# Attention of a decoder trunk: batched norms with their offset in PSUM, values as the standing operand in the last two tiles, and a split last projection

## The chip, the cores and the metric

The kernel runs on one core of a Trainium2 chip. The metric is the device time of one execution in microseconds; lower is better. The engines are named as in the profile: PE is TensorE, PEld its loads of the standing operand, DVE is VectorE, ACT is ScalarE, POOL is GpSimd, SP is SyncE. In a PE row the first operand after the arrow is the standing one or the moving one as the program lists it; what stands is said in words where it matters.

## The reference

Two layers over 1024 positions of width 1024. Layer 0 is sparse attention, layer 1 a gated linear recurrence; a dense feed-forward follows each. The change lies in the attention, in the norm behind it and at the entry to the first feed-forward.

```python
def attend_block(args):
    qb, qib, wb, start = args
    ...
    rel = jax.nn.relu(jnp.einsum('bqhd,bsd->bhqs', qib, k_idx))
    score = jnp.einsum('bqh,bhqs->bqs', wb, rel).astype(jnp.float32)
    ...
    _, sel = lax.top_k(score, topk)
    ...
    logits = jnp.einsum('bqgrd,bqkgd->bqgrk', qg, k_sel).astype(jnp.float32) * (ATT_HEAD_DIM ** -0.5)
    ...
    p = jax.nn.softmax(logits, axis=-1).astype(dt)
    o = jnp.einsum('bqgrk,bqkgd->bqgrd', p, v_sel)
...
    return out @ w_o
...
    h = layer_norm(DEEPNORM_ALPHA * h + mix, ln_g[layer, 0], ln_b[layer, 0])
    ffn = swiglu(h, ffn_w_gate[layer], ffn_w_up[layer], ffn_w_down[layer])
    h = layer_norm(DEEPNORM_ALPHA * h + ffn, ln_g[layer, 1], ln_b[layer, 1])
```

## The kernel before

The positions are cut into 8 tiles of 128 queries. `att_main` goes over them as j = 0 to 7; a tile has two groups (gi = 0, 1) of 8 heads, which share one key and one value head of 64 channels. Tile j attends to j + 1 blocks of 128 keys. The chosen keys (the top 256 of the index scores) enter as a bias of large numbers on the logits.

For each head, `head` does this:

- **Logits.** Two matmuls per 512 (or 384, 448) keys give `L` in PSUM (L1597). DVE adds the bias and takes the row minimum in one instruction (L1599), ACT takes the exponential and its sum (L1601).
- **Transposes.** PE turns the 128x128 blocks of `p`, up to four into one PSUM bank `T` (L1607). ACT copies the bank to SBUF as `pT` (L1609).
- **Product.** For each key block `pT` stands and the 64 channels of the values move (L1612), and the sum stays in bank `O`. The product is in plain fp32, which the trace shows as two PE instructions per product.

After 8 heads, `heads_out` divides by the sums (L1625, DVE), turns the 128x512 result (L1634, PE) and splits it into a rounded part and a rest (L222 on ACT, L223 on DVE), `oth` and `otl`. `att_out` is the output projection: two halves of 512 columns, for each 8 blocks of the contraction with three matmuls (`mm3`, L103 to L105), 48 in all, into bank `W`; then DVE adds the scaled residual (L1647). Then comes the norm of that tile: `layer_norm([j], *gb, True)`, of which the order is

```python
            if spread:
                nc.scalar.activation(r, r, AF.Identity, bias=mr[:, i : i + 1], scale=rs[:, i : i + 1])
                nc.gpsimd.tensor_tensor(r, r, g, op=ALU.mult)
                v.tensor_tensor(r, r, b, op=ALU.add)
```

that is, DVE takes the statistics (L128, L129) and an inverse root in eleven 128x1 operations (`rsqrt`, L111 to L116) and one more (L135), ACT scales and shifts (L139), POOL multiplies by the gain (L140), DVE adds the offset (L141).

`heads_out` and `att_out` are not called at once: they are put into the list `late` with a count, and `tick`, called after each head, lowers the counts and calls what has come to 0. A projection started by `tick` goes on two blocks of the contraction per head. `LATE[j]` is the count for the projection of tile j. Beside that, the index scores and the search for the top keys of later tiles (`index`, `find`, up to L1502) are mixed into the heads of tiles 0 to 5 by the numbers in `PLAN`; for tiles 6 and 7 these are zero. The tile framework fixes the buffers and the waits; each engine then runs its instructions in order. PSUM has two banks each for `L`, `T`, `O`, and the pools of banks `W` and `I` (the index scores).

Behind the last projection stands the entry to the feed-forward, `enter`: it turns the normed rows with PE (L339, four 128x128 blocks per bank `Y`), splits them (L457, L458) and starts the gate and up matmuls. For later feed-forwards there is already a form in which the norm's offset is added on PE: a matmul of the small tiles `blocks` and `off` onto the turned bank (L341), and at the end of that feed-forward the same offset for the residual (`plus`, L726).

## Time and profile before

| | |
|---|---|
| median of 3 runs | 2673.97 us (2669.08 to 2676.54) |
| profiled execution, own time | 2682.22 us |
| its span, first to last instruction | 2680.4 us |
| PE busy in it | 2542.1 us (95%) |
| DVE busy | 1978.4 us (74%) |
| ACT busy | 1124.5 us (42%) |
| POOL busy | 266.7 us (10%) |
| mean granted clock of PE | 0.972 |

The profiled execution is 8.25 us longer than the median. Busy time of PE counts matmuls that overlap in the pipeline at the length that the profile gives each, so a busy PE is not a PE at its peak; how far apart matmuls start (the pitch) is read from the timeline. In the trace of this kernel the first exponential of tile 0 is at 256 us, of tile 1 at 288, tile 5 at 474, tile 6 at 537, tile 7 at 601; the last matmul of the projection is issued at 691.6 and the entry to the feed-forward runs from there to 739.

### The profile page before, as it was taken

The numbers are of one execution on the slowest core, as the hardware profiler recorded it, in microseconds if no ns is written. First come the engines' busy times: TensorE is split into PE (matmuls) and PEld (weight loads), VectorE is DVE, ScalarE is ACT, GpSimd is POOL, SyncE is SP. The second block draws the span as 40 slices with busy tenths as digits, with TensorE's granted clock in tenths as the row PEclk, the third lists the DMA queues.
The fourth block names the chain that finished last, engine by engine and source line by source line (L and its number), as shares of the span: only waits on it lengthen the run. The fifth ranks groups of instructions, "written<-read, shape, count | busy, mean of one in ns | idle before, by whom it ended". The sixth has DMA issues, their size and how long they took to land.

```text
span 2680.4 us, 37329 instructions
## 1 busy us (share of the span) xinstructions
PE 2542.1 (95%) x13242; PEld 2115.5 (79%) x13242; DVE 1978.4 (74%) x4025; ACT 1124.5 (42%) x2192; POOL 266.7 (10%) x350
## 2 busy tenths in 40 slices
PE   8977799999899999999999999999899999999998
PEld 7765678888787888888878888888678878888786
DVE  6599889644577877656678888887786777665667
ACT  4576667555432223334444333333344323333431
POOL 1323522220000000000001221111000000000000
PEclk9987799999899999999999999999899999999999
DMA  3213210000166663276631111112525663326853
GB/s 132 79 56 128 92 36 28 25 33 17 40 203 227 227 207 112 93 244 209 209 134 48 40 71 56 40 52 87 185 107 187 223 229 111 118 86 214 271 181 126
DMA packets 160338, 332.59 MB, mean 124 GB/s; under 512 B 16712, under 2 KB 48152, under 8 KB 152472
## 3 DMA queue, kind: packets, MB, share of 16 engines
q1 hardware_dynamic: 160152, 330.21, 36.6%
q8 instruction: 104, 1.70, 0.3%
q14 instruction: 82, 0.67, 0.1%
HBM read 231.02 MB, written 99.09 MB: 123 GB/s over the span
## 4 chain that ended last, share of the span: by engine, by line
PE 61%; DVE 20%; DMA 11%; issue 4%; ACT 3%; SPq 1%; POOL 1%; DVEq 0%; ACTq 0%; POOLq 0%
PE M L103 8%; PE M L104 8%; PE M L105 7%; PE Y L103 6%; PE Y L105 6%; PE Y L104 5%; PE O L1612 4%; DMA wdt<-in_wd_dram 4%; DMA t4q<-wdt 3%; DVE w L458 3%; PE Y L1036 2%; PE L L1597 2%; PE T L1607 2%; DVE wdt L567 2%; PE Y L339 1%
## 5 line engine op out<-in xcount | busy, mean ns | idle before, releaser
L457 ACT CAST w<-raw 128x512 fp32r<-128x512 f32 (+1 forms) x373 | 288.1, 774 | 479.8 <-PE M L105 253.2
L458 DVE TENSOR_TENSOR w<-raw,w 128x512 fp32r<-128x512 f32 (+1 forms) x373 | 327.8, 882 | 167.0 <-ACT w L457 165.6
L103 PE MATMUL M<-x,w 128*128 128x512 f32 (+1 forms) x1120 | 435.4, 389 | 8.2 <-DVE e L491 6.4
L104 PE MATMUL M<-x,w 128*128 128x512 f32 (+1 forms) x1120 | 431.4, 385 | 0.0
L105 PE MATMUL M<-x,w 128*128 128x512 f32 (+1 forms) x1120 | 428.1, 383 | 3.5 <-DVE w L458 3.5
L103 PEld LDWEIGHTS M<-x,w 128*128 128x128 f32 x1120 | 212.7, 190 | 49.4 <-DVE e L491 8.5
L103 PE MATMUL Y<-x,w 128*128 128x512 f32 (+1 forms) x644 | 245.7, 381 | 6.1 <-DVE e L491 5.5
L105 PE MATMUL Y<-x,w 128*128 128x512 f32 (+1 forms) x644 | 245.5, 381 | 2.1 <-DVE w L458 2.1
L105 PEld LDWEIGHTS M<-x,w 128*128 128x128 f32 x1120 | 212.5, 190 | 42.7 <-DVE w L458 3.9
L104 PE MATMUL Y<-x,w 128*128 128x512 f32 (+1 forms) x644 | 245.4, 381 | 0.0
L457 ACT CAST w<-s 128x512 fp32r<-128x512 f32 x180 | 111.7, 621 | 312.2 <-PE M L105 99.0
L104 PEld LDWEIGHTS M<-x,w 128*128 128x128 f32 x1120 | 212.9, 190 | 36.5
L1612 PEld LDWEIGHTS O<-vv,pT 128*128 128x128 f32 x1152 | 148.1, 199 | 27.2 <-ACT pT L1609 24.1
L1612 PE MATMUL O<-vv,pT 128*128 128x64 f32 x1152 | 154.7, 282 | 5.1 <-ACT pT L1609 4.0
L458 DVE TENSOR_TENSOR w<-s,w 128x512 fp32r<-128x512 f32 x180 | 124.4, 691 | 42.6 <-ACT w L457 42.1
L103 PEld LDWEIGHTS Y<-x,w 128*128 128x128 f32 x644 | 121.5, 189 | 31.1 <-DVE e L491 7.2
L105 PEld LDWEIGHTS Y<-x,w 128*128 128x128 f32 x644 | 121.5, 189 | 25.6 <-DVE w L458 2.5
L104 PEld LDWEIGHTS Y<-x,w 128*128 128x128 f32 x644 | 121.4, 189 | 23.0
L1597 PE MATMUL L<-ks,qt 128*128 128x512 f32 (+5 forms) x384 | 115.7, 391 | 20.7 <-DVE nm L1599 19.6
L567 DVE TENSOR_TENSOR wdt<-wdt 128x512 f32<-128x512 f32 x104 | 71.8, 691 | 79.1 <-DMA wdt<-in_wd_dram 54.5
L1609 ACT COPY pT<-T 128x512 f32<-128x512 f32 (+3 forms) x192 | 85.2, 478 | 85.7 <-PE T L1607 84.9
L1601 ACT ACTIVATE p<-p,nm 128x128 f32<-128x128 f32 (+7 forms) x128 | 99.3, 777 | 51.0 <-DVE nm L1599 50.5
(426 smaller groups left out, 5484.5 us busy)
## 6 DMA issues: line engine op xcount, KB each, us to landing
raw<-in_wgu_dram SPq DMA_DIRECT2D x44, 1024.0 KB
wdt<-in_wd_dram SPq DMA_DIRECT2D x44, 512.0 KB
raw<-in_wd_dram SPq DMA_DIRECT2D x66, 256.0 KB
raw<-in_hw_dram SPq DMA_DIRECT2D x16, 1024.0 KB
qr<-qd SPq DMA_DIRECT2D x64, 128.0 KB
t5q<-wdt SPq DMA_DIRECT2D x26, 256.0 KB
t7q<-wdt SPq DMA_DIRECT2D x26, 256.0 KB
h7q<-s SPq DMA_DIRECT2D x26, 256.0 KB
```

The source lines that it names most:

```text
L103: mm(out, a[0], b[0], start=first, stop=False, **kw)
L104: mm(out, a[0], b[1], start=False, stop=False, **kw)
L105: mm(out, a[1], b[0], start=False, stop=last, **kw)
L457: self.nc.scalar.copy(hi, x)
L458: (eng or self.nc.vector).tensor_tensor(lo, x, hi.bitcast(F32), op=ALU.subtract)
L567: sub = lambda o, a, b: v.tensor_tensor(o, a, b, op=ALU.subtract)
L1036: nc.tensor.matmul(pl[rows, n, cols], lhs, rhs, start=True, stop=True)
L1597: nc.tensor.matmul(ps, s.qt[:, h % 4, :], s.ks[gi][i][:, kr], start=i == 0, stop=i == 1)
L1601: nc.scalar.activation(p, p, AF.Exp, bias=nm, scale=-1.0, accum_out=sm[:, h : h + 1])
L1607: nc.tensor.transpose(pt[:, i * P : (i + 1) * P], p[:, c : c + P], self.ident)
L1609: nc.scalar.copy(pT[:, : m * P], pt[:, : m * P])
L1612: nc.tensor.matmul(po[:, h * 64 : (h + 1) * 64], pT[:, i * P : (i + 1) * P], s.vv[:, k, gi * 64 : (gi + 1) * 64], start=k == 0, stop=k == j,)
```

## The change

It has five parts.

1. **Norms.** `layer_norm` works on a batch of tiles: 0 to 3 during tile 6, 4 and 5 during tile 7, 6 and 7 at the end, with one `rsqrt` per batch. DVE now subtracts the mean and multiplies by the gain in one instruction, and ACT multiplies by the inverse root (`Copy` with a scale). POOL's multiply and DVE's addition of the offset are gone. The offset goes into `enter` as matmuls onto the turned banks, 20 of them (12 rows of contraction, 512 columns), and into the end of the first feed-forward as `plus`, 48 more instructions of 128 columns. The parts of the offset are made once, in tile 1 (two loads, some small DVE operations).
2. **Values standing.** In tiles 6 and 7 (`WIDE = 6`) two heads are taken together. `values` builds for each key block 128 standing columns: the rounded values and their rest, 64 channels each (16 POOL operations). `mix` turns up to two key blocks of both heads into one bank `T`; ACT casts it (`hi`, in `pT`), DVE takes the rest (`lo`, in `rel` or `sc1`), and per key block the 256 columns of `hi` and then of `lo` move through the standing values, each in one instruction. `both` adds the two halves of the 128 result rows (ACT copy, DVE add) and turns them back, four 64x128 transposes per four heads, into a bank of the index scores.
3. **Last projection.** `att_last` has both column halves of tile 7's projection in the two banks of the logits; the 24 matmuls of the first group of heads are issued ahead of the turning of the second.
4. **Tile 6's projection** starts later: `LATE[6]` is 11 where it was 4.
5. **Index loads** come two heads at a time (4 loads where there were 8 per tile), and in the search a comparison and a multiply are one DVE instruction.

```diff
-    def layer_norm(self, ts, g, b, spread=False):
+    def layer_norm(self, ts, g):
...
+            yield
+        rs = self.rsqrt(mv[:, :, 1], n, 1.0, LN_EPS, "ln")
+        yield
         for i, t in enumerate(ts):
             r = self.resid[:, t, :]
-            if spread:
-                nc.scalar.activation(r, r, AF.Identity, bias=mr[:, i : i + 1], scale=rs[:, i : i + 1])
-                nc.gpsimd.tensor_tensor(r, r, g, op=ALU.mult)
-                v.tensor_tensor(r, r, b, op=ALU.add)
...
+            v.scalar_tensor_tensor(r, r, mv[:, i, 0:1], g, op0=ALU.subtract, op1=ALU.mult)
+            nc.scalar.activation(r, r, AF.Copy, scale=rs[:, i : i + 1])
+            yield
...
-                    self.operand(p, n, pairs[p], less[p % 2])
+                    self.operand(p, n, pairs[p], less[p % 2], self.off)
...
-    LATE = [10, 3, 3, 6, 8, 5, 4, 2]
+    LATE = [10, 3, 3, 6, 8, 5, 11]
...
             if k == KD - 1:
-                gb.extend(self.load_gb(g, b))
+                nc.sync.dma_start(gain, g.partition_broadcast(P))
+                self.off, self.plus = self.parts(self.gbp, b, "off", self.row()), b
...
+            if j == self.WIDE:
+                self.values()
+            if j >= NT - 2:
+                norms.append(self.layer_norm(((0, 1, 2, 3), (4, 5))[j - NT + 2], gain))
...
+                    if len(ps) == 2:
+                        if h % 4 == 1:
+                            accs.append(self.tile(s.psO, [P, 512], F32, "O"))
+                        self.mix(bp, j, gi, h // 2 % 2, ps, accs[-1])
+                        ps = []
+                        if h % 4 == 3:
+                            late.append([2, lambda h=h, a=accs: self.both(h // 4, a)])
...
-        while late or outs:
-            tick()
+        for e in late:
+            e[1]()
+        for x in outs + norms:
+            weave(x)
+        self.att_last((oth, otl), wo)
+        weave(self.layer_norm((6, 7), gain))
...
+    def values(self):
...
+        slots = ["high0", "low0", "high1", "high1", "low1", "low1", "sc0", "sc0"]
...
+            gp.tensor_copy(x[:, :, :64], vv)
+            gp.tensor_tensor(x[:, :, 64:], vv, x[:, :, :64].bitcast(F32), op=ALU.subtract)
...
+    def mix(self, bp, j, gi, i, ps, acc):
...
+        for k0 in range(0, j + 1, 2):
+            m = min(2, j + 1 - k0)
+            pt = self.tile(s.psT, [P, 512], F32, "T")
+            for k in range(m):
+                for e in range(2):
+                    c = (k0 + k) * P
+                    nc.tensor.transpose(pt[:, (2 * k + e) * P : (2 * k + e + 1) * P], ps[e][:, c : c + P], self.ident)
+            hi = self.tile(bp, [P, 512], F32R, "pT", bufs=3)
+            tag, bufs = (("rel", 2), ("sc1", 1))[k0 // 2 % 2]
+            lo = self.tile(s.sel, [P, 512], F32R, tag, bufs=bufs)
+            n = m * 256
+            nc.scalar.copy(hi[:, :n], pt[:, :n])
+            v.tensor_tensor(lo[:, :n], pt[:, :n], hi[:, :n].bitcast(F32), op=ALU.subtract)
+            for k in range(m):
+                for x in (hi, lo):
+                    y = x[:, k * 256 : (k + 1) * 256]
+                    first, last = k0 + k == 0 and x is hi, k0 + k == j and x is lo
+                    nc.tensor.matmul(o, s.vhl[k0 + k][:, gi, :], y, start=first, stop=last)
...
+    def both(self, i, accs):
...
+        nc.scalar.copy(x, acc[64:])
+        v.tensor_tensor(x, x, acc[:64], op=ALU.add)
...
+            nc.tensor.transpose(s.po[:, o : o + 64], x[:, h * P : (h + 1) * P], self.ident[:64, :64])
...
+    def att_last(self, o, wo):
+
+        pw = [self.tile(self.att.psL, [P, 512], F32, "L") for _ in range(2)]
+        cols = [slice(c * 512, (c + 1) * 512) for c in range(2)]
+        for ks in (range(4), range(4, 8)):
+            for c in range(2):
+                for k in ks:
+                    ws = tuple(w[:, cols[c]] for w in wo[k])
+                    self.mm3(pw[c], (o[0][:, k, :], o[1][:, k, :]), ws, k == 0, k == KD - 1)
```

The first place is PE in the middle of tile 7. Before, eight transposes of one head, its logits and the eight products of another follow each other; `T` is the turned bank, `O` the product, `L` the logits, `W` the projection of tile 6:

```order
L1607 MATMUL T_1784_7124<-ident_61,p_1779_7112 128x128 x4
L1607 MATMUL T_1786_7135<-ident_61,p_1779_7112 128x128 x4
L1597 MATMUL L_1800_7186<-ks10_5_72,qt_1725_6886 128x512
L1612 MATMUL O_1722_6881<-vv_7_74,pT_1785_7129 128x64 x4
L1612 MATMUL O_1722_6881<-vv_7_74,pT_1787_7140 128x64 x4
L1597 MATMUL L_1800_7186<-ks11_6_73,qt_1725_6886 128x512
L104 MATMUL W_1808_7224<-xl0_683_2977,oth_1638_6550 128x512
L105 MATMUL W_1808_7224<-xh0_681_2975,otl_1639_6551 128x512
```

After, logits of the next heads, a piece of `both` and a piece of the projection stand between the transposes of a bank and its products (L1635, where `high0`, `low0`, `high1` are the standing values, `pT` the rounded part and `rel` or `sc1` the rest that move):

```order
L1688 MATMUL L_1677_6730<-ks00_3_70,qt_1588_6422 128x512
L1688 MATMUL L_1677_6730<-ks01_4_71,qt_1588_6422 128x512
L1635 MATMUL O_1656_6659<-pT_1658_6665,high0_1369_5654 128x256
L1688 MATMUL L_1695_6796<-ks10_5_72,qt_1644_6623 128x512
L1688 MATMUL L_1695_6796<-ks11_6_73,qt_1644_6623 128x512
L1648 MATMUL I_1655_6654<-ident_61,sc2_1654_6651 128x64 x4
L103 MATMUL W_1725_6901<-xh1_611_2831,oth_1367_5652 128x512
L1635 MATMUL O_1656_6659<-rel_1659_6666,high0_1369_5654 128x256
L1635 MATMUL O_1656_6659<-pT_1658_6665,low0_1370_5655 128x256
L1635 MATMUL O_1656_6659<-rel_1659_6666,low0_1370_5655 128x256
L1635 MATMUL O_1656_6659<-pT_1661_6678,high1_1371_5656 128x256
L1624 MATMUL T_1663_6686<-ident_61,p_1642_6619 128x128
```

The products of a key block, one instruction of 64 columns per head and part before, are now one of 256 columns for two heads and a part, and the ones of the rest wait for a DVE subtraction.

The second place is PE at the end of attention. Before, the last products are followed by the turning of the second group (L1634) and only then by the second half of the projection's contraction (`xh1`, `xl1`):

```order
L1612 MATMUL O_1722_6881<-vv_7_74,pT_1803_7197 128x64 x4
L1612 MATMUL O_1722_6881<-vv_7_74,pT_1805_7208 128x64 x4
L1634 MATMUL O_1807_7217<-ident_61,qr_1806_7215 128x128 x4
L103 MATMUL W_1808_7224<-xh1_682_2976,oth_1638_6550 128x512
L104 MATMUL W_1808_7224<-xl1_684_2978,oth_1638_6550 128x512
L105 MATMUL W_1808_7224<-xh1_682_2976,otl_1639_6551 128x512
```

After, matmuls of the first half of the contraction (`xh0`, `xl0`, into `L`, both column halves) stand around the turning of `both` (L1648) and of `heads_out` (L1709):

```order
L103 MATMUL L_1795_7196<-xh0_610_2830,oth_1583_6415 128x512
L104 MATMUL L_1795_7196<-xl0_612_2832,oth_1583_6415 128x512
L105 MATMUL L_1795_7196<-xh0_610_2830,otl_1584_6416 128x512
L1648 MATMUL I_1754_7011<-ident_61,sc2_1791_7165 128x64 x4
L103 MATMUL L_1795_7196<-xh0_610_2830,oth_1583_6415 128x512
L104 MATMUL L_1795_7196<-xl0_612_2832,oth_1583_6415 128x512
L105 MATMUL L_1795_7196<-xh0_610_2830,otl_1584_6416 128x512
L103 MATMUL L_1795_7196<-xh0_610_2830,oth_1583_6415 128x512
L1709 MATMUL I_1793_7175<-ident_61,qr_1792_7173 128x128 x4
L104 MATMUL L_1795_7196<-xl0_612_2832,oth_1583_6415 128x512
L105 MATMUL L_1795_7196<-xh0_610_2830,otl_1584_6416 128x512
L103 MATMUL L_1794_7195<-xh1_611_2831,oth_1583_6415 128x512
```

The transposes that waited for DVE and ACT have matmuls in front of them that need neither.

The third place is DVE in the same tile 7. Before, the fused bias and minimum (L1599, two rows each) and a norm's offset (L141):

```order
L1599 ISA p_1779_7112,nm_1783_7121<-L_1782_7118,bias7_9_76,nm_1781_7116 128x512
L1599 ISA nm_1783_7121 128x1
L1599 ISA p_1788_7146,nm_1790_7150<-L_1789_7147,bias7_9_76 128x512
L1599 ISA nm_1790_7150 128x1
L141 TENSOR_TENSOR resid_680_2950<-resid_680_2950,gb_841_3468 128x1024
L1599 ISA p_1788_7146,nm_1792_7155<-L_1791_7152,bias7_9_76,nm_1790_7150 128x512
L1599 ISA nm_1792_7155 128x1
```

After, two subtractions per pair of banks (L1630) and the addition of `both` (L1643) stand between the same operations (L1690 now):

```order
L1690 ISA p_1669_6712,nm_1671_6716<-L_1670_6713,bias7_9_76 128x512
L1690 ISA nm_1671_6716 128x1
L1630 TENSOR_TENSOR rel_1638_6599<-T_1636_6593,pT_1637_6598 128x512
L1630 TENSOR_TENSOR sc1_1641_6612<-T_1639_6606,pT_1640_6611 128x512
L1690 ISA p_1669_6712,nm_1673_6721<-L_1672_6718,bias7_9_76,nm_1671_6716 128x512
L1690 ISA nm_1673_6721 128x1
L1690 ISA sc3_1674_6724,nm_1676_6728<-L_1675_6725,bias7_9_76 128x512
L1690 ISA nm_1676_6728 128x1
L1643 TENSOR_TENSOR sc2_1654_6651<-sc2_1654_6651,O_1602_6464 64x512
L1630 TENSOR_TENSOR rel_1659_6666<-T_1657_6660,pT_1658_6665 128x512
L1630 TENSOR_TENSOR sc1_1662_6679<-T_1660_6673,pT_1661_6678 128x512
L1690 ISA sc3_1674_6724,nm_1678_6733<-L_1677_6730,bias7_9_76,nm_1676_6728 128x512
```

Each subtraction waits for a cast on ACT, and the fused operation behind it, which feeds the exponential, waits in turn.

## Rows read from the trace of the kernel before

**Rows 1.** Busy time by stretch; columns as in the first line, PEclk the granted clock.

```profile
core 0: us, PE busy (x) PEld busy (x) DVE busy (x) ACT busy (x) POOL busy (x), PEclk, DMA share, GB/s
255.00:289.00 34.00, 25.71 (x91) 20.09 (x92) 29.76 (x79) 22.69 (x71) 17.35 (x11) 0.50 0.27 85
288.00:474.00 186.00, 166.65 (x1047) 140.79 (x1047) 165.88 (x477) 132.20 (x312) 51.45 (x42) 0.95 0.14 43
537.00:601.00 64.00, 63.99 (x443) 55.53 (x442) 29.98 (x95) 34.76 (x66) 12.77 (x10) 1.00 0.08 25
601.00:673.00 72.00, 70.92 (x489) 61.26 (x489) 30.40 (x87) 37.25 (x66) 7.02 (x6) 1.00 0.07 23
692.00:713.00 21.00, 14.67 (x88) 13.09 (x87) 16.94 (x34) 10.77 (x18) 2.54 (x1) 0.76 0.35 125
```

**Rows 2.** Waits in tiles 1 to 4: total us, times, longest.

```profile
PE L L1597 <- DVE nm L1599: 12.6, 16, 2.8
```

**Rows 3.** Timeline, PE in the tail of attention.

```profile
679.23 0.66 PE L1634 MATMUL O<-ident,qr 128*128 128x128 f32 x4 [0.78 <-DVE qr L1625]
...
680.56 0.50 PE L103 MATMUL W<-xh,oth 128*128 128x512 f32 x1 [0.68 <-ACT oth L222]
...
686.22 0.50 PE L103 MATMUL W<-xh,oth 128*128 128x512 f32 x1 [0.78 <-DVE resid L1647]
...
691.55 0.39 PE L105 MATMUL W<-xh,otl 128*128 128x512 f32 x1
```

**Rows 4.** Timeline at the feed-forward's entry: DVE during the last multiply, then PE.

```profile
700.05 2.84 DVE L474 TENSOR_TENSOR s<-s,raw 128x512 f32<-128x512 f32 x1
...
703.55 0.48 PE L339 MATMUL Y<-ident,resid 128*128 128x128 f32 x1 [3.78 <-DVE x L458]
```

**Rows 5.** Timeline, tile 7: start, length, engine, line, operation, count.

```profile
606.61 1.89 PE L1612 MATMUL O<-vv,pT 128*128 128x64 f32 x16
...
608.34 1.04 PE L1607 MATMUL T<-ident,p 128*128 128x128 f32 x8
...
609.22 0.60 PE L1634 MATMUL O<-ident,qr 128*128 128x128 f32 x4
```

**Rows 6.** Timeline, matmuls with 256 moving columns in the feed-forward's entry.

```profile
714.26 0.28 PE L103 MATMUL M<-x,w 128*128 128x256 f32 x1
...
714.38 0.28 PE L104 MATMUL M<-x,w 128*128 128x256 f32 x1
```

**Rows 7.** Group of the products on PE, tiles 6 and 7 (537 to 692 us).

```profile
L1612 PE MATMUL O<-vv,pT 128*128 128x64 f32 x492 | 61.5, 277 | 1.4 <-ACT pT L1609 0.6
```

**Rows 8.** Timeline, `plus` in the last feed-forward.

```profile
1934.00 1.06 PE L726 MATMUL M<-plus,blocks 12*128 12x128 bf16 x16
```

**Rows 9.** Groups of DVE instructions, tiles 6 and 7 (537 to 692 us).

```profile
L223 DVE TENSOR_TENSOR otl<-O,oth 128x512 fp32r<-128x512 f32 x5 | 3.4, 686 | 1.4 <-ACT oth L222 1.4
L116 DVE SCALAR_TENSOR_TENSOR ln1y<-ln1t,ln1y 128x1 f32<-128x1 f32 x9 | 1.4, 158 | 0.2
```

**Rows 10.** Timeline, end of tile 7: transposes, copy, product; in brackets the idle time before.

```profile
675.11 1.04 PE L1607 MATMUL T<-ident,p 128*128 128x128 f32 x8
675.81 1.07 ACT L1609 COPY pT<-T 128x512 f32<-128x512 f32 x2 [2.10 <-PE T L1607]
...
676.44 0.77 PE L1612 MATMUL O<-vv,pT 128*128 128x64 f32 x5 [0.29 <-ACT pT L1609]
```

**Rows 11.** Groups of the whole span: the norm's multiply on POOL.

```profile
L140 POOL TENSOR_TENSOR resid<-resid,gb 128x1024 f32<-128x1024 f32 x8 | 19.2, 2397 | 81.8 <-ACT resid L139 78.6 <-issue 3.2
```

**Rows 12.** Timeline, DVE during such a multiply in tile 2.

```profile
337.70 2.33 DVE L1481 TENSOR_TENSOR hik<-hik,negl 128x2 f32<-128x2 f32 x1
```

**Rows 13.** Timeline, offset matmuls of a later entry, four transposes between.

```profile
1332.41 0.39 PE L341 MATMUL Y<-blocks,off 12*128 12x512 bf16 x1
...
1333.31 0.39 PE L341 MATMUL Y<-blocks,off 12*128 12x512 bf16 x1
```

**Rows 14.** Timeline, `plus` in the recurrence's output projection.

```profile
1913.84 1.86 PE L726 MATMUL M<-plus,blocks 12*128 12x128 bf16 x16 [1.10 <-DMA plus<-t]
```

More of the change, by code (lines that the diff above doesn't have):

```diff
@@ L1537, in tick @@
                     e[1]()
-            if outs and next(outs[0], self) is self:
-                outs.pop(0)
+            for x in (outs, norms):
+                if x and next(x[0], self) is self:
+                    x.pop(0)
         owed = [0.0, 0.0]
@@ L1618, in head, with logits, heads_out @@
                 )
-    def heads_out(self, bp, gi, po, sm, oth, otl):
-        nc, v = self.nc, self.nc.vector
+    def logits(self, bp, j, gi, h, bias, sm, p):
+        nc, v, s = self.nc, self.nc.vector, self.att
+        nch, n = self.chunks(j)
+        S = nch * n
+        hh = gi * 8 + h
+        if h % 4 == 0:
+            s.qt = s.ahead
+        if h % 4 == 0 and (j, hh // 4) != (NT - 1, 3):
+            s.ahead = self.queries(bp, *((j, hh + 4) if hh < 12 else (j + 1, 0)))
+        p = p[:, :S]
+        nm = 3.0e38
+        for c in range(nch):
+            kr = slice(c * n, (c + 1) * n)
+            ps = self.tile(s.psL, [P, 512], F32, "L")[:, :n]
+            for i in range(2):
+                nc.tensor.matmul(ps, s.qt[:, h % 4, :], s.ks[gi][i][:, kr], start=i == 0, stop=i == 1)
+            least = self.tile(bp, [P, 1], F32, "nm", bufs=6)
+            v.tensor_tensor_reduce(p[:, kr], ps, bias[:, kr], 1.0, nm, ALU.add, ALU.min, accum_out=least)
+            nm = least
+        nc.scalar.activation(p, p, AF.Exp, bias=nm, scale=-1.0, accum_out=sm[:, h : h + 1])
+    def heads_out(self, bp, j, gi, po, sm, oth, otl):
+        nc, v, s = self.nc, self.nc.vector, self.att
+        po, pool, tag = (po, s.psO, "O") if j < self.WIDE else (s.po, s.psI, "I")
         v.reciprocal(sm, sm)
```

113 lines of the change are left out of this document (57 added, 56 removed).

## Prediction

> **What bounds the kernel now.** I read the stretches first, then inside tiles 6 and 7 the groups, the timeline for pitches, and the waits. In [rows 1] the attention falls into two kinds of stretch. In tiles 1 to 4 (288 to 474 us) DVE is busy 165.88 of 186 us (89%), and PE waits for it: 12.6 us for the row minimum of the logits [rows 2]. In tiles 6 and 7 (537 to 673 us) PE is busy for nearly the whole time at full clock, and DVE for only 29.98 of 64 and 30.40 of 72 us (44%). So in tiles 6 and 7 the time is the sum of PE's instruction starts, and DVE has room; in tiles 1 to 4 the work of DVE has a price. Behind them comes a tail in which PE waits three times, .78, .68 and .78 us, for a chain of DVE and ACT [rows 3], and at the entry to the feed-forward a wait of 3.78 us [rows 4] in a stretch with a granted clock of 0.76 [rows 1].
>
> Since matmuls overlap, I take pitches and not lengths. Sixteen product instructions start at 606.61 and the next transposes at 608.34: .108 us each. Eight transposes until 609.22: .11 each [rows 5]. With 256 moving columns the pitch is .12 (714.26 to 714.38) [rows 6]. With 512 it is (691.55 - 686.22)/23 = .232 [rows 3].
>
> **Tiles 6 and 7: values standing.** Tile 6 has 7 key blocks and 16 heads, tile 7 has 8: 240 products, two instructions each, 480 (the group has 492, 12 of them left from tile 5 [rows 7]). They go: 480 x .108 = 51.8 us. New are 2 instructions per pair of heads and key block, (7 + 8) x 8 x 2 = 240 at .12 = 28.8. The 240 transposes stay. `both` adds 32 transposes of 64 columns; between the 1.06/16 = .066 of the offset's short matmuls [rows 8] and the .11 of a full transpose they cost 2.1 to 3.5; I take 3. PE's sum: -51.8 + 28.8 + 3 = -20 us.
>
> [...] I go by the rows: what bounds an old product is the same at 64 and at 128 moving columns, .108 against .11 [rows 5].
>
> DVE's price: each bank of transposes now needs a rest. Tile 6 has 8 pairs x 4 banks and tile 7 the same: 64 banks, 56 full (.686 us, the price of the same split in `heads_out` [rows 9]) and 8 of half the width (.34): 41.1 us. `both` adds 8 operations of at most .686: 5.5. The small operations of two norms go, 2 x 12 x .158 = 3.8 [rows 9]. DVE comes to 60.4 + 41.1 + 5.5 - 3.8 = 103 us, in some 134 us: 77%. It does not become the bound by its sum. Its latency matters: from the first transpose to the first product it was 676.44 - 675.11 = 1.33 us [rows 10]; the product of the rest needs a subtraction more, 2.0 us. In the order's first place there lie between the start of a bank's transposes and the product of its rounded part four transposes (.44), four logits (.93), a product of another bank (.12), four short transposes (.3), a projection matmul (.23) and three products (.36): 2.4 us; without projection and `both` 1.85, and the rest's product comes two later. So the bare chain is just covered. What isn't covered is a subtraction that queues on DVE behind a fused bias and minimum. The stretch with 89% of DVE loses 12.6 of 186 us of PE to that, 6.8% [rows 2]; the one with 44% none. For 77% I take half, 3.4% of 134 us, rounded down, +4 (bounds 0 and 9). ACT has 34.76 of 64 us and only swaps copies for casts of like size. `values` costs POOL 16 operations of an eighth of the multiply's width (2.397/8 = .3 us [rows 11]), 4.8 us, hidden beside the logits of the first two heads and needed one block at a time; uncovered it would be at most 4.8, which is in the upper end.
>
> **The tail.** The first two waits of [rows 3] (.78 + .68) get 24 matmuls of the first half in front, 5.6 us of cover, of which the longer chain with `both` (ACT copy, DVE add, four transposes, some 2 us) uses a part. The third, .78 for the residual between two column halves, goes since each half has its own bank. I take -2 us. Tile 6's projection, started 7 heads later, is 48 matmuls that have to be done anyway; it only fills. **B, tiles 6, 7 and tail: -20 + 4 - 2 = -18 us (-22 to -13).**
>
> **Tiles 1 to 5.** Four norms lose twelve small operations each, 4 x 12 x .158 = 7.6 us, and one batch of eleven comes back (1.7). A big DVE operation stays for a big one: the offset's addition goes, mean and gain come. A 128x2 operation of DVE that took 2.33 us during POOL's multiply [rows 12] comes back to .16: 2.2 us. The offset's parts add seven small operations of .16 to .69 us; I take 2.5. Index loads and the merged comparison I take at nothing: their cover is the 2 loads ahead and DVE's sum, and if it is gone it is within this part's bounds. The sum is -5.6; DVE is 89% busy, so nearly all counts. **A: -5 us (-9, with a second such multiply blocked as at the entry, to 0).**
>
> [...]
>
> **Entry.** Removed: POOL's multiply between the last norm and the first split; DVE's 2.84 us was 2.15 above the .69 of its size, and PE's 3.78 us of wait hangs on it [rows 4]. Added: the offset on PE. Two offset matmuls start .90 us apart with four transposes (.44) between [rows 13], so one costs .46 with the bubbles around it; 20 cost 9.2 us. One or two stand where PE waits for weights, -1.5. The last norm now serves two tiles in DVE (1.2 us more ahead of the first split). Of the 3.78 us and the stretch at 0.76 (a quarter of 21 us) I credit 5. **C: 9.2 - 1.5 - 5 = +3 us (-4, if stall and clock both come back and the matmuls fill waits, to +8).**
>
> **End of the first feed-forward.** 48 more instructions of `plus` at 1.06/16 = .066 or less: **D: +3 us; 7 if they wait as once in the recurrence (1.10 [rows 14]) at half clock.**
>
> **The sum.** -18 - 5 + 3 + 3 = -17 us on the execution's own 2682.2: 2665. It lies 8.25 us above the median of the runs, so the forecast is 2657.
>
> **The rivals.**
> *The rest's chain stalls PE (slower).* Tiles 6 and 7, place: the wait of a product (L1635) for DVE's subtraction (L1630). With two banks of transposes and the fused operations in the same queue, a subtraction that finds one of them ahead (.69 + .08) loses that less what the 2.4 us leave, some .5 us; on 64 banks 32 us instead of 4: 2657 + 28 = 2685. It decides at .33 us a bank (21 us): there the change is worth nothing. For it: the fused operation waits in turn for logits, as in [rows 2]. Against it: the cover worked out above, and 23% of DVE free. Chance 0.10.
> [...] Chance 0.04.
> *More comes back.* No wait in tiles 6 and 7 (-22), DVE's full relief (-9), stall and clock at the entry return (-4), `plus` at 2.7: -32, 2642. For it: PE had 3.78 us there that only DVE's late split explains. Chance 0.18.
> *The offset takes it back.* B -13, A 0, C +8, D +7: +2, 2676; half of that way is likelier, around 2668. For it: in the later entry nothing hid them (.90 instead of .44 [rows 13]). Chance 0.14.
> *Half clock in tiles 6 and 7.* [...] The change makes PE less busy there. [...] Chance 0.06.
> That the parts don't happen isn't a case: the order shows them.
>
> **How the numbers follow.** The forecast case has 0.48 and its own range 2649 to 2665. A measurement of this kernel can tell about 0.3%, 8 us: faster is below 2666, slower above 2682. Faster: 0.48 + 0.18 + 0.06 of the offset's case = 0.72; same: 0.08 + 0.06 + 0.02 of a milder stall = 0.16; slower 0.12. The range goes from the fuller gain, 2641, to the dearer offset, 2676; beyond it lie the stall, the gap, and a piece of the gain, 0.2.
>
> **What would show it.** After: tiles 6 and 7 and the tail in some 136 us of 155; the product's group 240 instructions at a pitch near .12; DVE about 77% busy there; waits of L1635 for L1630 below 9 us in sum; clock 1.00. The first split's wait at the entry below 3.78; 20 offset matmuls .46 apart from the transposes. If the waits for L1630 exceed 21 us, or the last two tiles take 150 us, the forecast fails by the chain; if the entry is 8 us longer, by the offset; if the stretches before tile 6 get longer, by something that I don't see.

## The result, and the profile after

The changed kernel takes 2635.65 us (median of 4 runs, 2631.06 to 2639.33) beside 2675.26 us of the kernel before (2669.08 to 2677.19). The ratio is 0.9855 with a 95% interval of 0.9831 to 0.9879: 39 us less, between 32 and 45. The forecast was 2657 with a range from 2641 to 2676: right in sign, and much too small a gain. A later run of the same program (experiment e13, whose edit moved nothing) had 0.9875 (0.9852 to 0.9897), so 33 to 39 us is the size to explain. The profiled execution has a span of 2632.1 us, mean granted clock 0.978. The two profiled spans differ by 48.3 us, more than the medians do, since the profiled execution of the kernel before lay 8.25 us above its median.

Busy time by stretch of the changed kernel comes first, with the columns of [rows 1]. The stretches run between the first exponentials of tiles, which are now at 252.8 us (tile 0), 287.1 (tile 1), 462.0 (tile 5), 526.4 (tile 6) and 582.3 (tile 7); the entry's first transpose is at 657.6.

```profile
core 0: us, PE busy (x) PEld busy (x) DVE busy (x) ACT busy (x) POOL busy (x), PEclk, DMA share, GB/s
252.80:287.10 34.30, 23.93 (x89) 18.86 (x90) 31.69 (x81) 22.64 (x71) 17.93 (x11) 0.57 0.25 81
287.10:462.00 174.90, 162.63 (x1041) 139.42 (x1039) 158.34 (x425) 125.34 (x304) 42.95 (x41) 0.96 0.12 35
526.40:582.30 55.90, 55.49 (x351) 46.60 (x352) 44.15 (x110) 33.47 (x67) 7.64 (x8) 1.00 0.06 15
582.30:657.60 75.30, 73.46 (x456) 60.55 (x454) 56.16 (x127) 45.85 (x80) 3.82 (x4) 1.00 0.07 22
657.60:677.00 19.40, 17.97 (x134) 14.79 (x132) 17.70 (x39) 12.59 (x21) 0.00 (x0) 1.00 0.34 120
```

The reader is to see three things. In tiles 6 and 7 DVE went from under half to 44.15 of 55.9 us (79%) and 56.16 of 75.3 (75%), and PE still has hardly any gap. The clock is 1.00 through the end of attention and the start of the entry, where [rows 1] had 0.76. And tile 0 still runs at 0.57.

The products in the timeline (start, length), where [rows 5, 6] had .108 per old instruction and .12 for 256 columns:

```profile
599.95 0.28 PE L1635 MATMUL O<-pT,high 128*128 128x256 f32 x1
600.07 0.28 PE L1635 MATMUL O<-sc,high 128*128 128x256 f32 x1
600.19 0.27 PE L1624 MATMUL T<-ident,p 128*128 128x128 f32 x1
600.30 0.27 PE L1624 MATMUL T<-ident,sc 128*128 128x128 f32 x1
```

Products are .12 apart, transposes .11. And the groups of the products in tiles 6 and 7 (526.4 to 657.6), with the idle time before them at the end:

```profile
L1635 PE MATMUL O<-pT,high 128*128 128x256 f32 x48 | 14.7, 308 | 0.9 <-ACT pT L1629 0.7
L1635 PE MATMUL O<-pT,low 128*128 128x256 f32 x48 | 14.7, 306 | 1.1 <-ACT pT L1629 0.5
L1635 PE MATMUL O<-rel,low 128*128 128x256 f32 x48 | 13.2, 289 | 0.0
L1635 PE MATMUL O<-sc,high 128*128 128x256 f32 x32 | 9.4, 315 | 0.0
```

All products together waited 2.0 us, and those of the rest (`rel`, `sc`) not at all.

By stretch, in us, between the first exponentials and to the entry's first and last transposes. "Tile 7" includes the tail. The lower rows are the experiments below; each is one profiled execution.

| kernel | tiles 0 to 5 | tile 6 | tile 7 | entry | ratio to before (95%) |
|---|---|---|---|---|---|
| before | 280.3 | 64.6 | 90.4 | 47.1 | 1 |
| changed | 273.6 | 55.9 | 75.3 | 45.6 | 0.9855 (0.9831 to 0.9879) |
| e13, the same program in effect | 267.1 | 55.9 | 75.3 | 47.0 | 0.9875 (0.9852 to 0.9897) |
| e1, values moving | 265.6 | 62.1 | 86.6 | 45.5 | 0.9928 (0.9912 to 0.9944) |
| e2, tail and tile 6's projection as before | 273.7 | 55.9 | 85.4 | 47.0 | 0.9906 (0.9890 to 0.9922) |
| e10, only tile 6's projection as before | 273.6 | 55.9 | 81.2 | 45.5 | 0.9889 (0.9870 to 0.9908) |
| e3, norms as before | 277.9 | 56.7 | 81.9 | 47.1 | 0.9915 (0.9896 to 0.9933) |
| e6, norm per tile without POOL | 276.4 | 59.1 | 78.8 | 43.2 | 0.9867 (0.9844 to 0.9889) |
| e4, offset on DVE | 267.8 | 56.0 | 78.6 | 44.9 | 0.9827 (0.9806 to 0.9848) |
| e9, index and search as before | 267.8 | 55.9 | 75.3 | 47.0 | 0.9871 (0.9851 to 0.9892) |
| e11, values standing alone | 280.0 | 56.6 | 91.8 | 47.1 | 0.9960 (0.9945 to 0.9974) |
| e12, projection alone | 278.2 | 67.2 | 85.3 | 46.1 | 0.9977 (0.9966 to 0.9988) |
| e14, offset on DVE, old index | 267.8 | 56.2 | 77.0 | 43.6 | 0.9842 (0.9823 to 0.9861) |

Two things help in reading it. Tiles 6 and 7 repeat to 0.1 us where their code is the same (e9, e13 and the changed kernel), so they can be compared by one profile. Tiles 0 to 5 do not: the changed kernel and e13 have 273.6 and 267.1 with the same instructions in the same order. The ratios have intervals of 3 to 6 us to either side. A loss "by time" below is taken against the 0.9855 of the changed kernel; against the 0.9875 of e13 each of them is 5 us smaller, so the stretches are the better measure.

One sentence ahead of the prediction is wrong: `W` in the first place of the order before (`W_1808`, tile 7) is tile 7's own projection, of which a first part was already mixed into its last heads; tile 6's was over by then. No number of the prediction rests on it.

### The profile page after: what moved, and what is told of

Its sections match the earlier page's. It is cut to its first block, busy times and chain, and to the rows that moved or that the text cites. A ratio compares the mean times of both kernels' runs of the same rounds, so it can differ in the third digit from the quotient of the medians.

```text
span 2632.1 us, 36939 instructions
## 1 busy us (share of the span) xinstructions
PE 2515.4 (96%) x13102; PEld 2090.3 (79%) x13102; DVE 2013.9 (77%) x4042; ACT 1129.7 (43%) x2176; POOL 250.0 (9%) x334
## 4 chain that ended last, share of the span: by engine, by line
PE 62%; DVE 12%; DMA 8%; issue 3%; ACT 2%; SPq 1%; POOL 0%; DVEq 0%; ACTq 0%; POOLq 0%
PE M L105 9%; PE M L103 9%; PE M L104 9%; PE Y L103 6%; PE Y L104 6%; PE Y L105 6%; DMA wdt<-in_wd_dram 3%; PE Y L1023 3%; DMA t4q<-wdt 2%; DVE w L445 2%; PE O L1664 2%; PE L L1688 2%; PE Y L326 2%; DVE wdt L554 1%; PE O L1635 1%
## 5 line engine op out<-in xcount | busy, mean ns | idle before, releaser
L445 DVE TENSOR_TENSOR w<-s,w 128x512 fp32r<-128x512 f32 x180 | 124.5, 692 | 42.2 <-ACT w L444 41.7
L103 PE MATMUL M<-w 128*128 128x512 f32 x288 | 113.6, 398 | 6.5 <-DVE rows L744 4.7
L104 PE MATMUL M<-w,w 128*128 128x512 f32 x288 | 113.5, 394 | 0.2 <-DVE w L445 0.2
L105 PE MATMUL M<-w,w 128*128 128x512 f32 x288 | 113.6, 395 | 0.0
L1692 ACT ACTIVATE p<-p,nm 128x128 f32<-128x128 f32 (+7 forms) x120 | 90.8, 757 | 38.2 <-DVE nm L1690 35.6
```

The lines of the kernel that those rows point to most:

```text
L103: mm(out, a[0], b[0], start=first, stop=False, **kw)
L104: mm(out, a[0], b[1], start=False, stop=False, **kw)
L105: mm(out, a[1], b[0], start=False, stop=last, **kw)
L445: (eng or self.nc.vector).tensor_tensor(lo, x, hi.bitcast(F32), op=ALU.subtract)
L1692: nc.scalar.activation(p, p, AF.Exp, bias=nm, scale=-1.0, accum_out=sm[:, h : h + 1])
```

## The experiments

In all of them the rest is the changed kernel, unless it says otherwise. The first question was which part gives what.

**e1, values moving.**

```diff
-    WIDE = 6
+    WIDE = 8
```

> The changed kernel with the values moving again in tiles 6 and 7 (WIDE = 8); norms, split last projection and held-back projection of tile 6 stay. Theory A (the products' PE time was sized right at -22 us, and the rest's chain costs no wait): 22 to 26 of the 39 us are lost, ratio to the kernel before 0.994, the time from tile 6's first exponential to the last projection matmul about 154 us instead of 131. Rival B (the rest's chain eats a good part, and the gain came from the norms and the tail): at most 12 us are lost, ratio 0.990 or lower.

Measured: 2653.7 us, ratio 0.9928, 20 us of the change's gain lost. Tiles 6 and 7 take 148.7 us instead of 131.2, which is 17.5 us more. That lies between A and B, a little nearer to A, and close to the -16 that the prediction's terms give for the values by themselves (-20 for PE's starts, +4 for waits).

**e2, tail and held-back projection as before.**

```diff
-    LATE = [10, 3, 3, 6, 8, 5, 11]
+    LATE = [10, 3, 3, 6, 8, 5, 4, 3]
...
-            if j < NT - 1:
-                late.append([self.LATE[j], lambda j=j, o=(oth, otl): outs.append(self.att_out(j, o, wo))])
+            late.append([self.LATE[j], lambda j=j, o=(oth, otl): outs.append(self.att_out(j, o, wo))])
...
-        self.att_last((oth, otl), wo)
```

> The changed kernel with tile 7's projection made as the other tiles' (no split) and tile 6's projection after 4 heads as before. Theory A (the tail was sized right, -2 us, or a little more since a stretch of half clock goes with its waits): 2 to 5 us lost, ratio 0.9865 to 0.9875; the time from the last product to the entry's first transpose about 13 us instead of 11. Rival B (the held-back projection is what fills the waits of tiles 6 and 7): 8 us or more lost, ratio 0.9885 or higher, most of it inside tile 7.

Measured: 2647.77 us, 0.9906: 14 us lost by time; by stretches 10.1 in tile 7 (85.4 instead of 75.3) and 1.4 at the entry. B's size. The term of -2 us for the tail, with nothing for the held-back projection, is refuted.

**e10, only the held-back projection undone** (split kept).

```diff
-    LATE = [10, 3, 3, 6, 8, 5, 11]
+    LATE = [10, 3, 3, 6, 8, 5, 4]
```

> The changed kernel with tile 6's projection after 4 heads as before; tile 7's stays split. Theory A (of the 12 us of tail and held-back projection together, half is the filling of the bare chain in the last heads of tile 7): 4 to 7 us lost, ratio 0.987 to 0.988, with waits of .2 to .4 us for cast and subtraction at the last banks. Rival B (all of it is the split: waits and half clock in the tail): at most 2 us lost, ratio 0.985 to 0.9863.

Measured: 2642.72 us, 0.9889: 9 us lost by time, 5.9 in tile 7 (81.2). The stretch is

```profile
581.10:662.30 81.20, 75.67 (x456) 60.10 (x455) 56.34 (x128) 45.78 (x80) 3.82 (x4) 1.00 0.06 20
```

With the same number of matmuls as in 582.30 to 657.60 above (x456), PE has 5.5 us without one instead of 1.8, and its busy time grows by 2.2 (a product that had to wait is shown with .38 us in the rows of e11 below, one in a row with .28). PE's longer waits in tiles 6 and 7 (total us, times, longest) are

```profile
PE O L1635 <- ACT pT L1629: 1.6, 6, 0.5
PE L L1688 <- DVE nm L1690: 1.3, 3, 0.6
PE I L1709 <- DVE qr L1700: 0.8, 1, 0.8
PE O L1635 <- DVE rel L1630: 0.7, 2, 0.3
```

and .7 and .3 us more, 5.4 in all, where the changed kernel has 1.4. Only 1.1 of the 4.0 us more stand ahead of products; the rest stands ahead of logits, of the turning of `both` and of the last heads, and of the projection. So A has the size by the stretch, and its place in part. Of the 10 us of e2 the hold (the later start of tile 6's projection) is worth about 6 and the split (of the last projection) 4.

**e3, norms as before**: each tile's own, multiply on POOL, offset added by DVE, nothing of the offset on PE.

```diff
-            nc.scalar.activation(r, r, AF.Copy, scale=rs[:, i : i + 1])
+                nc.scalar.activation(r, r, AF.Identity, bias=mr[:, i : i + 1], scale=rs[:, i : i + 1])
+                nc.gpsimd.tensor_tensor(r, r, g, op=ALU.mult)
+                v.tensor_tensor(r, r, b, op=ALU.add)
...
-                self.off, self.plus = self.parts(self.gbp, b, "off", self.row()), b
+                self.off = self.plus = None
```

> The changed kernel with each tile's norm as before (multiply on POOL, offset added by DVE, none of it on PE). Theory A (what was under-sized is the relief of DVE in tiles 1 to 5 and the return of stall and clock at the entry): 10 to 15 us lost, ratio 0.9895 to 0.991; tiles 1 to 5 about 9 us longer, the entry with a wait of some 4 us and half clock again, the first feed-forward's end 3 us shorter. Rival B (norms are worth what was predicted, nothing net; tiles 1 to 5 differed by chance): within 3 us of the changed kernel, ratio 0.985 to 0.987.

Measured: 2651.29 us, 0.9915: 16 us lost by time, A's size. The wait at the entry that A names is there, and tiles 0 to 5 are 4 us longer than in the changed kernel and 11 longer than in e13. But 7.3 us stand in tiles 6 and 7, of which A says nothing. The timeline of e3 there, at the start of tile 7 and at its end:

```profile
587.64 2.40 POOL L140 TENSOR_TENSOR resid<-resid,gb 128x1024 f32<-128x1024 f32 x1 [3.40 <-ACT resid L139]
...
590.07 1.23 DVE L141 TENSOR_TENSOR resid<-resid,gb 128x1024 f32<-128x1024 f32 x1 [0.82 <-POOL resid L140]
...
591.68 0.39 PE L1645 MATMUL O<-sc,sc 128*128 128x256 f32 x1 [1.21 <-DVE sc L1640]
...
657.20 2.38 POOL L140 TENSOR_TENSOR resid<-resid,gb 128x1024 f32<-128x1024 f32 x1 [41.49 <-ACT resid L139]
...
657.70 0.68 DVE L1653 TENSOR_TENSOR sc<-sc,O 64x512 f32<-64x512 f32 x1 [1.92 <-ACT sc L1652]
...
659.37 0.40 PE L105 MATMUL L<-xh,otl 128*128 128x512 f32 x1
659.61 1.22 DVE L141 TENSOR_TENSOR resid<-resid,gb 128x1024 f32<-128x1024 f32 x1 [1.23 <-POOL resid L140]
660.75 0.68 DVE L1710 TENSOR_TENSOR qr<-I,sm 128x512 f32<-128x512 f32 x1
...
661.49 0.66 PE L1719 MATMUL I<-ident,qr 128*128 128x128 f32 x4 [1.72 <-DVE qr L1710]
...
662.82 0.80 PE L103 MATMUL L<-xh,oth 128*128 128x512 f32 x1 [0.68 <-ACT oth L222]
...
663.41 0.63 PE L104 MATMUL L<-xl,oth 128*128 128x512 f32 x1
663.84 0.63 PE L103 MATMUL L<-xh,oth 128*128 128x512 f32 x1
```

At the end of the tile the offset of tile 6's norm (L141, 1.22 us) had waited for POOL's multiply, and the division of the last heads (L1710) queued behind it on DVE. At its start the offset of tile 5's norm had done the same to a subtraction of the new chain (L1640), and a product stood 1.21 us. At the end PE stood 1.72 us, then .68, and its matmuls went on slower (512 columns .43 apart, .23 before; the granted clock was 0.78 from 660 to 665 us and 0.88 from 665 to 670). At the entry the whole pattern of [rows 4] is back:

```profile
678.25 2.84 DVE L473 TENSOR_TENSOR s<-s,raw 128x512 f32<-128x512 f32 x1
...
681.74 0.47 PE L339 MATMUL Y<-ident,resid 128*128 128x128 f32 x1 [3.78 <-DVE x L457]
```

**e4, offset on DVE**, batched norms kept.

```diff
             nc.scalar.activation(r, r, AF.Copy, scale=rs[:, i : i + 1])
+            v.tensor_tensor(r, r, self.shift, op=ALU.add)
             yield
...
-                self.off, self.plus = self.parts(self.gbp, b, "off", self.row()), b
+                self.off = self.plus = None
```

> The changed kernel with batched norms, but the offset added by a DVE operation of 128x1024 per tile behind ACT's scaling; no offset matmuls at the entry and no plus in the first feed-forward. Theory A (20 offset matmuls cost 9 us and plus 3 us of PE, DVE's ten us of additions cost little in tiles 6 and 7 but 2.5 us ahead of the entry): 4 to 8 us gained on the changed kernel, ratio 0.9825 to 0.984. Rival B (the late additions bring back a wait at the entry and with it the half clock): 0 to 6 us lost, ratio 0.9855 to 0.988.

Measured: 2628.6 us, 0.9827, the fastest kernel here. A's size: 7 us less than the changed kernel, though the intervals overlap. Tile 7 is 3.3 us longer, with waits of .84 and .67 us in the tail where the changed kernel has one of .21; no addition stands ahead of that division, and why PE waits there is not shown. Tile 0 takes 31.5 us without the parts of the offset and 34.4 with them (the changed kernel and e13). The entry is 44.9 us, hardly shorter without its 20 matmuls, since PE's waits are back there in part:

```profile
PE Y L327 <- ACT gb L361: 3.3, 1, 3.3
PE Y L327 <- DVE x L445: 2.0, 1, 2.0
```

**e6, norm after each projection, without POOL.**

```diff
+            v.scalar_tensor_tensor(r, r, mv[:, i, 0:1], g, op0=ALU.subtract, op1=ALU.mult)
...
-                nc.scalar.activation(r, r, AF.Identity, bias=mr[:, i : i + 1], scale=rs[:, i : i + 1])
-                nc.gpsimd.tensor_tensor(r, r, g, op=ALU.mult)
+                nc.scalar.activation(r, r, AF.Copy, scale=rs[:, i : i + 1])
                 v.tensor_tensor(r, r, b, op=ALU.add)
```

(The minus lines are those of the norm before, as in e3.)

> The changed kernel with a norm after each projection as before, but without POOL: DVE subtracts the mean and multiplies by the gain in one operation, ACT scales, DVE adds the offset; no offset on PE. It has eight DVE operations of 1.25 us more than the norm of before and the same small ones. Theory A (what cost was POOL's multiply, which holds DVE up): close to the batched norms with the offset on DVE, at most 6 us above 2628.6, ratio 0.9827 to 0.985; no half clock and no long wait at the entry. Rival B (what cost was the late place: small operations in the stretches that DVE bounds, and one more norm between the projection and the entry): as with the norms of before or longer, 2648 to 2658, ratio 0.9905 or higher.

Measured: 2635.74 us, 0.9867. It lies between: 13 us better than e3 though DVE has eight operations of 1.25 us more, and 11 us worse than the batched norms with the offset on DVE (e4). So both theories seem to hold for a half: the way over POOL costs about as much as the early place of the small operations. By stretches most of the latter is in tiles 0 to 5 (276.4 against 267.8), where one profile tells no more than some 6 us, and the profiled execution of e6 (2646.89 us) lay 11 us above its median.

**e9, index loads and search as before.** The diff is the change's part 5 taken back.

> The changed kernel with index loads of one head and the search's comparison and multiply apart, as before. Theory A (tile 1 and the stretch ahead of tile 0 are shorter for these): 4 to 7 us lost, ratio 0.987 to 0.988. Rival B (as predicted, nothing; the earlier start of tile 0 is chance): within 2 us, ratio 0.985 to 0.9865.

Measured: 2636.68 us, 0.9871. By its number that is A's range, but the changed program itself has 0.9855 and 0.9875, so there is nothing that these runs can tell, as predicted.

The second question was why tail and hold are worth so much. For that the values and the projection were tried by themselves, with norms as before.

**e5, values standing as the only edit.** It was built from the changed kernel by taking the other parts back.

```diff
-    LATE = [10, 3, 3, 6, 8, 5, 11]
+    LATE = [10, 3, 3, 6, 8, 5, 4, 3]
...
-        self.att_last((oth, otl), wo)
-        weave(self.layer_norm((6, 7), gain))
+        self.layer_norm([NT - 1], *gb, True)
```

> The kernel before with the values standing in tiles 6 and 7 as the only edit (norms, projections, index loads and search as before; the last projection's count is 3 so that it comes behind the turning). Theory A (the parts add up): it gives what it took to undo it, 18 to 20 us, ratio 0.9925 to 0.993. Rival B (it needs the held-back projection: without it the chain from transposes through cast and subtraction lies bare at the end of tile 7, some 4 us, and the tail has a longer chain, 2 us): 10 to 14 us, ratio 0.995 to 0.996, with waits of the products for cast and subtraction in each of the last banks.

Measured: 2669.38 us, 0.9995. By a slip of mine it norms tile 7 twice (the last line is one too many), and its entry took 54.7 us instead of 47.1, so its time isn't that of the edit. Tile 6 took 56.6 us and tile 7 91.9.

**e11, the same with one norm.**

```diff
-        self.layer_norm([NT - 1], *gb, True)
```

> As the run with the values standing alone, without its second norm of tile 7, which lay ahead of the entry and made it 54.7 us long instead of 47.1. Theory A (interplay: alone the values win 8 us in tile 6 and nothing in tile 7): 6 to 9 us faster than the kernel before, ratio 0.9965 to 0.9978; tile 6 56.6 us, tile 7 with the tail 90 to 92, entry 47. Rival B (the second norm also lengthened the tail, and the values alone are worth the predicted 16 us): ratio 0.994, tile 7 with the tail at most 85.

Measured: 2663.03 us, 0.9960: 11 us. Tile 6 with 56.6 and tile 7 with 91.8 us come out as A has it; the time is 2 to 5 us better than A's, which the stretches up to the entry (7 us) don't explain. The end of tile 7 in e11, with the waits in brackets:

```profile
662.69 1.07 ACT L1634 CAST pT<-T 128x512 fp32r<-128x512 f32 x2 [1.71 <-PE T L1629]
663.31 0.69 DVE L1635 TENSOR_TENSOR sc<-T,pT 128x512 fp32r<-128x512 f32 x1 [1.60 <-ACT pT L1634]
663.33 0.38 PE L1640 MATMUL O<-pT,high 128*128 128x256 f32 x1 [0.29 <-ACT pT L1634]
...
664.05 0.39 PE L1640 MATMUL O<-sc,high 128*128 128x256 f32 x1 [0.34 <-DVE sc L1635]
...
666.26 0.38 PE L1640 MATMUL O<-pT,sc 128*128 128x256 f32 x1 [0.67 <-ACT pT L1634]
666.99 0.39 PE L1640 MATMUL O<-sc,sc 128*128 128x256 f32 x1 [0.34 <-DVE sc L1635]
...
669.00 0.46 PE L1653 MATMUL I<-ident,sc 64*128 64x64 f32 x4 [1.39 <-DVE sc L1648]
...
670.24 1.12 PE L1714 MATMUL I<-ident,qr 128*128 128x128 f32 x4 [0.78 <-DVE qr L1705]
...
672.03 0.79 PE L103 MATMUL W<-xh,oth 128*128 128x512 f32 x1 [0.68 <-ACT oth L222]
```

Each bank waits for its cast and then for its subtraction, .3 to .7 us each, because no other matmul is left to issue: the projection of tile 6 ended at 646 us. Over tiles 6 and 7 the products wait 6.8 us here by their groups (2.0 in the changed kernel), and the two longest of these waits (1.06 us in tile 6, 1.20 in tile 7) stand behind a norm's offset (L141), as in e3. Then `both`, division and split follow, 1.39 + .78 + .68 us, and PE slows down (the four transposes of L1714 take 1.12 us, those of the changed kernel, below, .60; the granted clock over tile 7 is 0.96, in the changed kernel 1.00). At the same place the changed kernel has:

```profile
647.26 0.28 PE L1635 MATMUL O<-sc,sc 128*128 128x256 f32 x1
...
649.32 0.46 PE L1648 MATMUL I<-ident,sc 64*128 64x64 f32 x4
...
650.74 0.60 PE L1709 MATMUL I<-ident,qr 128*128 128x128 f32 x4
...
652.02 0.50 PE L103 MATMUL L<-xh,oth 128*128 128x512 f32 x1 [0.21 <-ACT oth L209]
```

**e12, split and held-back projection alone**, values moving, norms as before (the diffs of e1 and e3 together).

> The changed kernel with norms as before and the values moving: beside the index loads and the search, the split last projection and the held-back projection of tile 6 are what is left. Theory A (they pay by filling the bare chain that the standing values make): tiles 6 and 7 with the tail at 149 to 153 us against 155.0 before, 148.5 with the values alone and 138.5 with both, so that the two together give more than their sum; ratio 0.995 to 0.997. Rival B (they pay by themselves, some 10 us): 143 to 146 us, ratio 0.992.

Measured: 2666.74 us, 0.9977: 6 us, and 152.5 us in tiles 6 and 7. A. With the norms of before the four cases of tiles 6 and 7 are then 155.0 us (neither), 148.4 (values alone), 152.5 (projection alone) and 138.5 (both, e3). One gives 6.6, the other 2.5, both together 16.5.

The same runs tell what the batched norms are worth in tiles 6 and 7. With values standing it is 7.1 us without hold and split (148.4 in e11, 141.3 in e2) and 7.3 with them (138.5 in e3, 131.2 in the changed kernel). With values moving it is 3.8 (152.5 in e12, 148.7 in e1). That fits the rows of e3 and e11, where products of the new chain wait behind a norm's offset in DVE's queue.

**e13, parts of the offset in tile 6.**

```diff
-                self.off, self.plus = self.parts(self.gbp, b, "off", self.row()), b
...
                 self.values()
+                self.off, self.plus = self.parts(self.gbp, b, "off", self.row()), b
```

> The changed kernel with the parts of the offset made at the start of tile 6 instead of tile 1. Theory A (DVE, which bounds the first tiles, has its small operations and their waits there: 34.4 and 35.8 us against 31.5 and 33.3 where there are none): 4 to 6 us gained on the changed kernel, ratio 0.983 to 0.984, tiles 0 and 1 at 31.5 and 33.3. Rival B (the two stretches differ for another reason, or the operations cost as much in tile 6): no more than 2 us, ratio 0.985 or higher.

Measured: 2637.84 us, 0.9875; inconclusive, because nothing moved. In the trace the parts stand where they stood, from 248.8 us on, and the instructions of the two kernels stand in the same order on PE, DVE, ACT and POOL. What it gives is a repetition of the changed kernel: 0.9855 and 0.9875 for the same instructions.

**e14, offset on DVE and old index loads** (e4 and e9 together).

> The batched norms with the offset added by DVE, and index loads and search as in the kernel before. Theory A (by the stretches, tiles 2, 3 and 5 were 1.4, 2.5 and 0.8 us shorter with the old loads): 3 to 5 us gained on the 2628.6 of the run with the new loads, ratio 0.981. Rival B (the old loads lose what they lost in the time of their own run, 4 us): ratio 0.984.

Measured: 2630.47 us, 0.9842: B. Between 2628.6 and 2630.5 the runs don't tell. The two kernels with the offset on DVE have 0.9827 and 0.9842, the two of the changed program 0.9855 and 0.9875; so the offset matmuls are likelier a loss than a gain of this change, by 3 to 13 us, 8 by the means. From tile 0 to the end of the entry the four stretches sum to 444.6 and 447.2 us with the offset on DVE and to 445.3 and 446.0 on PE (e13, e9), no difference; behind the entry the former are about 4 us shorter, and there `plus` stands.

## Why the prediction was wrong, point by point

**What bounds the kernel.** Right: in tiles 6 and 7 the time is the sum of PE's starts (PE busy 55.49 of 55.9 and 73.46 of 75.3 us), and the added DVE work found room (77% forecast, 79% and 75% measured).

**Products.** Right in price: .12 for each of 240 instructions, where 480 at .108 went, and no clock loss in these tiles (1.00 in both; half clock there had a chance of 0.06). e1 shows the worth: the values' standing saves 17.5 us in tiles 6 and 7. The chance of 0.04, and the gap that lies beyond the range, stand for the opposite, 256 columns taking more of PE's time than the products of 64 did; no run shows it. That the same thing bounds a product of 64 moving columns and a transpose of 128 was my inference from .108 and .11 [rows 5]; by what either is bounded no run shows.

**Waits of the chain, +4 us.** Within its bounds, but wrong as one number. It is 2.0 us where other matmuls fill the chain and 6.8 where none do at the end of the tile (e11). The slower rival's mechanism, a subtraction that finds another operation ahead of it in DVE's queue, is there, far below its 28 us; what stood ahead in the longest waits was a norm's offset and not the fused operation that the rival named. The forecast's cover of 2.4 us a bank, taken from one place in the middle of tile 7, was carried to the end of tile 7, where there is none without the held-back projection.

**The tail, -2 us, and the held-back projection at "it only fills": one step that failed.** Undoing both costs 10 us in tile 7 (e2), of which the hold is 6 (e10). I priced the tail by the waits that the kernel before had ([rows 3], 2.2 us) and not by those that the new products bring with them. The parts don't add up: -6.6 and -2.5 apart, -16.5 together. The values by themselves give 9 less than the 16 forecast for them, and the projection with them 8 more than its 2, so by luck of signs the forecast of -18 for both was near what they give together, and this miss is not what made the total wrong.

**Norms, -5 + 3 + 3: the step that made the total wrong.** I forecast +1 us for them; undoing them costs 11 to 16 us by time (e3). I had counted eleven small operations per norm and one blocked DVE operation, all of it in tiles 1 to 5, and had given the norms no price in PE's time in tiles 6 and 7. There they are worth 7.3 us: in e3 a norm's offset stood in DVE's queue ahead of a subtraction and ahead of the division for which PE waited, and the granted clock fell after it (0.78 from 660 to 665 us). PE has 3.6 us more without a matmul, and its matmuls show 3.7 us more. That is a queue's effect, not a sum's.

In tiles 0 to 5 the sum was about right: DVE's instructions of the norms take 23.7 us before and 16.7 after, the parts add 2.4, and the blocked operation went from 2.33 to .16 us, -6.8 in all for the -5.6 forecast. The time moved by more. All five kernels with the norms of before have 277.9 to 280.3 us there (e5 has 280.0), all eight with batched norms 265.6 to 273.7, so 4 to 15 us, 9 or 10 by the means. By what waits it exceeds the sum is not shown. The batches also stand elsewhere than the order of the code says: statistics and gain (L128, L135) stay behind each tile's projection, and the first four scalings on ACT stand at 480 to 486 us, in tile 5.

**DVE beside POOL's multiply.** Two DVE operations took far longer during a multiply than elsewhere: 2.33 us in [rows 12], where the same line (L1481) took .16 its two other times, and 2.84 in [rows 4], where the median of its line (L474, 60 times) is .69; e3 has 2.84 there again. Both have their two inputs in SBUF (`hik` and `negl`, `s` and `raw`). Beside the six other multiplies of the kernel before, DVE's operations had their usual lengths: the fused bias and minimum, which reads bank `L`, .49 to .75 us, and the search's comparison (L1449) 1.27 and 1.28. Beside the multiply of 657.20 us in e3 an addition with an operand in bank `O` took .68, as in the changed kernel. So the rows show two lengthened operations, 2.2 us each, and no more than these to come back in DVE's own time. What taking POOL out gives (13 us between e3 and e6, 6 by stretches) may also come from the chain ACT, POOL, DVE getting shorter; no run parts the two.

**Entry, +3 us.** Measured -1.5 (-0.1 in e13). The matmuls cost about what was said (see below), but stall and half clock gave back more than the 5 us credited: over the whole entry PE's waits went from 6.5 to 1.4 us, and its clock from 0.89 to 1.00 (0.96 in e13, which is what its 1.4 us more go with). The forecast's -1.5 for matmuls that stand in a wait has no row behind it.

```profile
661.71 0.59 PE L328 MATMUL Y<-blocks,off 12*128 12x512 bf16 x2 [1.35 <-DVE blocks L371]
...
692.88 0.27 PE L326 MATMUL Y<-ident,resid 128*128 128x128 f32 x1
693.08 0.39 PE L328 MATMUL Y<-blocks,off 12*128 12x512 bf16 x1
693.40 0.33 PE L326 MATMUL Y<-ident,resid 128*128 128x128 f32 x1
```

In this piece of the changed kernel's entry an offset matmul takes .32 until the next start and delays its own by .09 (.20 after a transpose instead of .11): .41, forecast .46. The wait of 3.78 us is gone; 1.35 us for the constant `blocks` is new.

**End of the first feed-forward, +3 us.** About right. The 48 instructions of `plus` stand in three groups of 16, at 1178.9, 1240.3 and 1309.5 us. The first:

```profile
1178.88 1.06 PE L713 MATMUL Y<-plus,blocks 12*128 12x128 bf16 x16
1179.88 0.50 PE L103 MATMUL M<-w 128*128 128x512 f32 x1
```

The matmul ahead of it starts at 1178.56 and others follow each other by .23, so the group costs 1.1 us, the second 1.35. The third stands between the second entry's start and the third's end, where it is 84.0 us instead of 82.4: +1.6. That is some 4 us in all.

**The sum.** By stretches: tiles 0 to 5 -6.7 (-13.2 in e13), tiles 6 and 7 -23.8, entry -1.5 (-0.1), `plus` +4, in all -28 us (-33) where -17 was forecast. The rest to the measured 33 to 39 lies in the stretch ahead of tile 0 (tile 0 starts 3.7 us earlier, 5.7 in e13) and in the feed-forwards, whose code is otherwise the same and which differ by several us between kernels that do not touch them; what it is stays open. The rival "more comes back" (2642, chance 0.18) was the nearest, with the right places for the entry and for tiles 1 to 5, and the wrong one for tiles 6 and 7: its -22 there was to come from no wait of the chain, and it came in good part from the norms.

## What to carry to other kernels

When a change makes a chain longer, look at the end of the loop as well as its middle: here nothing was left to fill it (6.8 us of waits in e11 against 2.0), and independent work held back for that place was worth more than it gives alone (9.9 us by hold and split with the values standing, 2.5 with them moving). Do not price a tail by the waits that it has before the change. And when an operation leaves an in-order queue, ask which one stood behind it: in e3 one 1.22 us addition ahead of the last division cost PE a wait of 1.72 us, and the matmuls behind it were .43 apart instead of .23.

## What the runs showed of the hardware that was not expected

The same instructions in the same order took 273.6 and 267.1 us for tiles 0 to 5 in two profiles, while tiles 6 and 7 took 55.9 and 75.3 us in both. Tile by tile the difference lies in tile 1 (35.8 and 33.2 us at a granted clock of 0.89 in both), tile 3 (46.6 at 0.93 and 44.1 at 1.00) and tile 5 (64.3 at 0.95 and 62.9 at 0.97). Tile 0 took 34.4 us in both at 0.57, and tiles 2 and 4 took 42.2 and 50.3 us in both at 1.00. So here one profile was enough to compare stretches that ran at 1.00 in both, and elsewhere a difference of 6 us over six tiles tells nothing by itself.
